# Retention outputs by three products of 64 columns, two heads in one PSUM bank, and the pooled low parts on GpSimd

## Chip, cores and metric

One core of one Trainium2 chip runs the whole kernel in one launch. The metric is the device time of the launch in microseconds (us), the median of the runs. The engines are TensorE (PE for its matmuls, PEld for its weight loads), VectorE (DVE), ScalarE (ACT), GpSimd (POOL), and SyncE (SP), which issues most transfers.

## The reference, cut to what matters

The reference is a two-layer backbone. Each layer projects the tokens into three head groups (retention, latent attention, pooling), joins them by an output projection, and runs a gated MLP with a depthwise convolution. There are 1024 latent tokens and 256 context tokens; the last layer has outputs for latent tokens alone. The part in question is retention, with 4 heads of key width 32 and value width 64:

```python
def step(s, inp):
    qi, ki, vi = inp
    a = jnp.einsum('bhqd,bhkd->bhqk', qi, ki) * dmat
    o = jnp.einsum('bhqk,bhkv->bhqv', a, vi) + jnp.einsum('bhqd,bhdv->bhqv', qi * q_dec, s)
    ...
fwd = retention_chunkwise(q, k, v, log_gf, s_f, True)
bwd = retention_chunkwise(jnp.flip(q, 2), jnp.flip(k, 2), jnp.flip(v, 2), log_gb, s_b, False)
...
o = o * lax.rsqrt(jnp.mean(o * o, axis=-1, keepdims=True) + NORM_EPS)
return (merge_heads(o) * jax.nn.silu(g.astype(jnp.float32))).astype(g.dtype)
```

## The kernel before

All large products run on values that are split into a high and a low part (fp32r), so that one product of two values is a sum of several matmuls. The layers follow one another, and in each layer the stages follow in the order of the code: projections, retention states, `retention(l)`, attention, output projection, MLP. Instructions stay on each engine in the order in which the code issues them; the framework adds the semaphore waits that the tiles' readers and writers need.

`retention(l)` (L1511) works in **units**, one for a head h and a block j of 256 query tokens. Units come in pairs that share j: the even head first, the odd head second. Layer 0 has 20 units (16 with j < 4, and 4 of context tokens with j = 4, which have no state part), layer 1 has 16. Unit u issues, in this order:

- `low(u+1)` (L1555): the low part of the next unit's decayed scores, on GpSimd for an odd u+1, on VectorE for an even one.
- the output matmuls into a PSUM tile O: 4 with the states as weights (O<-qd, L1600) and 4 with the values as weights (O<-Ahl, L1605). The weights have 128 columns, the 64 high ones beside the 64 low ones, so that O has the products with the high halves in partitions 0 to 63 and those with the low halves in 64 to 127.
- `qk(u+2)`: two score matmuls (L1540) and on VectorE the product with the decay table into af (L1543).
- if one is left, one of five pieces of `values` (six matmuls of 512 columns into vps, L1287; then ve on ScalarE, L1292, and on VectorE, L1293).
- at u = 6 (`POOL0`) `pooled()` puts ten splits of the pooled outputs into a list (`later`); each call of `tick` runs as many of them as its credit pays for (1.5 a unit, and a split costs 0.6). A split is a copy on ScalarE (yp, L178) and a subtraction on VectorE (yp, L179).
- `ot` (L1623): ScalarE copies partitions 64 to 127 of O; `high(u+2)` (L1552) makes the next scores' high part on ScalarE; then VectorE adds the two halves of O into `ops` (L1626).
- after the odd head of a block, `finish` queues the block's norm: steps of squares and gate (acc L458 on ScalarE, L1565 on GpSimd), sums (rps, two matmuls or more, L138), roots (rs, L148 and L151), spread (Rps, eight matmuls for 512 tokens, L159), `out` and `low`. One step runs per unit, with the gaps that `FINW` lists behind each step.

PSUM tiles of `self.pu` (O, qk, vps) rotate over six banks. The attention stage begins (SL) when the last units' `out` is there.

Of the kernel before, what the change touches and what calls it, by code (L numbers as in the profile page):

```python
# [8 lines left out]
F32 = mybir.dt.float32  # L9
F32R = mybir.dt.float32r  # L10
AF = mybir.ActivationFunctionType
ALU = mybir.AluOpType
# [15 lines left out]
CH_LAT = [(0, 512), (512, 512)]  # L28
SEG_ALL = [(0, SEQ), (SEQ, CTX)]
SEG_LAT = [(0, SEQ)]  # L30
FINW = (0, 0, 1, 0, 0, 0)
POOL0 = 6

LAST = [(0, 512), (512, 256), (768, 256)]
# [127 lines left out]
class Net:  # L162
# [1348 lines left out]
    def retention(self, l):  # L1511
        nc = self.nc
        gv, v, R = self.gv, self.v, self.ret
        lat = l == L - 1
        Tq, chq = self.Tq, self.chq
        NJ = Tq // 256
        Y = self.Y = [None] * 16

        def pooled():

            for i in range(2):
                Y[6 + i], Y[14 + i] = (self.slot(s + i, [128, Tq], F32R, "yp") for s in (6, 14))
                for c0, n in chq:
                    self.later(0.6, lambda i=i, c0=c0, n=n: self.split(Y[6 + i][:, c0:c0 + n], Y[14 + i][:, c0:c0 + n],
                                                                       self.yp[:, i, c0:c0 + n]))

        js = (0, 1, 2, 3) + ((4,) if not lat else ())
        units = [(h, j) for i in range(2) for j in js for h in (2 * i, 2 * i + 1)]
        ops = [None, None]
        NU = len(units)  # L1530

        af, A = {}, {}

        def qk(u):
            h, j = units[u]
            q, k = R.st[h]
            ps = self.pu.tile([128, 512], F32, tag="up", name="qk")
            for i in range(2):
                c = (2 * j + i) * 128
                nc.tensor.matmul(ps[:, i * 256:i * 256 + 256], k[:, c:c + 128], q[:, j * 256:j * 256 + 256],  # L1540
                                 start=True, stop=True)
            af[u] = gv.tile([128, 512], F32, tag="sq", name="af", bufs=2)
            nc.vector.tensor_tensor(out=af[u], in0=ps, in1=R.D[h], op=ALU.mult)  # L1543

        def high(u):
            if u % 3 == 2 and u >= NU // 2 + 5:

                self.run_to(1, pool_end)
                A[u] = self.gva.tile([128, 2, 512], F32R, tag="A", name="Ahl")
            else:  # L1550
                A[u] = self.slot((22, 23, 16)[u % 3], [128, 2, 512], F32R, "Ahl")
            nc.scalar.activation(A[u][:, 0], af[u], AF.Copy)  # L1552

        def low(u):
            (nc.gpsimd if u % 2 else nc.vector).tensor_tensor(out=A[u][:, 1], in0=af.pop(u),  # L1555
                                                              in1=A[u][:, 0].bitcast(F32), op=ALU.subtract)

        def finish(i, c0, n):
            cs = slice(c0, c0 + n)
            t = {}  # L1560
            def sq():
                t["x"] = x = ops[i][:, cs]
                acc = self.sumsq([x], n, gv)
                t["r"] = Rms(self, acc, n, 1.0 / 64, R.sel)
                nc.gpsimd.tensor_tensor(out=x, in0=x, in1=self.gate[:, i, cs], op=ALU.mult)  # L1565
            def out():
                nc.vector.tensor_tensor(out=t["x"], in0=t["x"], in1=t["r"].R, op=ALU.mult)
                if Y[i] is None:
                    Y[i], Y[8 + i] = (self.slot(s, [128, Tq], F32R, "yr") for s in (i, 8 + i))
                nc.scalar.activation(Y[i][:, cs], t["x"], AF.Copy)  # L1570
            def low():
                nc.vector.tensor_tensor(out=Y[8 + i][:, cs], in0=t["x"], in1=Y[i][:, cs].bitcast(F32), op=ALU.subtract)
            st = [sq, lambda: t["r"].sums(), lambda: t["r"].roots(), lambda: t["r"].spread(), out, low]
            fins.append([f for f, w in zip(st, FINW) for f in [f] + [None] * w])

        def fin_step():

            for f in list(fins):
                g = f.pop(0)
                if g:  # L1580
                    g()
                if not f:
                    fins.remove(f)
        fins = []

        qk(0)
        high(0)
        qk(1)
        high(1)
        low(0)  # L1590
        for u, (h, j) in enumerate(units):
            if u + 1 < NU:
                low(u + 1)
            O = self.pu.tile([128, 512], F32, tag="up", name="O")[:, 0:256]
            first = True
            if j < 4:
                r = slice(32 * h, 32 * h + 32)
                for d in range(2):
                    for p in range(2):
                        nc.tensor.matmul(O, R.S[d][j // 2][r, j % 2].rearrange("p s e -> p (s e)"),  # L1600
                                         R.qd[d][p][r, j * 256:j * 256 + 256], start=first, stop=False)
                        first = False
            for p in range(2):
                for i in range(2):
                    nc.tensor.matmul(O, v[:, 2 * j + i, h], A[u][:, p, i * 256:i * 256 + 256], start=first,  # L1605
                                     stop=p == 1 and i == 1)
                    first = False
            if u + 2 < NU:
                qk(u + 2)
            if self.values:  # L1610
                self.values.pop(0)()
                if not self.values:
                    R.stack(2)
                    R.stack(3)
            if u == POOL0:
                pooled()
                pool_end = self.added[1]
            self.tick(1.5)
            i = h // 2
            if ops[i] is None:  # L1620
                ops[i] = self.slot((17, 13)[i], [128, Tq], F32, "op")
            t = gv.tile([64, 256], F32, tag=("krt", "kr2")[u % 2], name="ot")
            nc.scalar.activation(t, O[64:128], AF.Copy)  # L1623
            if u + 2 < NU:
                high(u + 2)
            nc.vector.tensor_tensor(out=ops[i][64 * (h % 2):64 * (h % 2) + 64, j * 256:j * 256 + 256], in0=O[0:64],  # L1626
                                    in1=t, op=ALU.add)
            if h % 2 == 1:

                if j == 4 or j > 1 and lat and i:  # L1630
                    finish(i, j * 256, 256)
                elif j % 2:
                    finish(i, j * 256 - 256, 512)
            fin_step()
        self.run_all()
        while fins:
            fin_step()


    def attention(self, l):  # L1640
# [4 lines left out]
        with ExitStack() as es:  # L1645
# [143 lines left out]
            def av(u, g):  # L1789
                s = st[u]  # L1790
                v = heads[units[u][0]][2]
                if g == 0:
                    s.O = self.b([128, 512], "O")
                if g < 2 and not units[u][2]:
                    return
                f = 8 if not units[u][2] else 0
                for k in ((0, 1, 2, 3), (4, 5, 6, 7), (8, 9))[g]:
                    nc.tensor.matmul(s.O[:, 0:256], v[:, k], s.ph[:, k], start=k == f, stop=False)  # L1798
                    nc.tensor.matmul(s.O[:, 0:256], v[:, k], s.pl[:, k], start=False, stop=k == 9)  # L1799
# [480 lines left out]
```

## Time and profile before

| what | us |
|---|---|
| median of 3 runs | 3344.43 |
| the runs | 3340.59, 3344.43, 3345.43 |
| the profiled execution's own time | 3334.97 |
| its span | 3333.2 |
| PE busy in it | 3171.5 (95%) |
| DVE busy | 2143.8 (64%) |
| ACT busy | 1291.3 (39%) |
| POOL busy | 413.1 (12%) |

Times of single instructions come from the profiled execution, which was 9.46 us below the median. The retention units lie at about 416 to 493 us (layer 0) and 2150 to 2213 us (layer 1) of its span. A PE row of several matmuls (x4) gives the time from the first's start to the last's end; matmuls are pipelined, so the distance of two starts, and not one's duration, is what one costs in a dense stream.

### The profile page before, as it was taken

To read this page: it belongs to the slowest core of one execution; us is meant where nothing else is said; L and a number is where in the kernel's file an instruction comes from. 1 tells how busy PE (TensorE), PEld (TensorE's weight loads), DVE (VectorE), ACT (ScalarE), POOL (GpSimd) and SP (SyncE) were. 2 spreads that over 40 slices of the span, in tenths; PEclk is the share of its full clock that TensorE was granted. 3 is DMA by queue.
4 is the path that set the end of the run, shared out by engine and by line. 5 is a ranking of instruction groups with operands and counts; after the bars stand their busy time and mean duration, and the time that the engine had idled before them with its cause. 6 is when DMAs were issued, how large, how long until landed. Compare 5 with 4: busy or idle time off the path is not lost.

```text
span 3333.2 us, 43486 instructions
## 1 busy us (share of the span) xinstructions
PE 3171.5 (95%) x16873; PEld 2676.0 (80%) x16873; DVE 2143.8 (64%) x3720; ACT 1291.3 (39%) x2277; POOL 413.1 (12%) x557
## 2 busy tenths in 40 slices
PE   7989789999999999999999899789999999999998
PEld 4767668998878888888888787579988788888887
DVE  6434768987667666666665745669985655555556
ACT  7443447774332222222222423457762422222222
POOL 3550221121310000000000300221112100000000
PEclk8999869999999999999999999879999999999999
DMA  6531643222212222222221322542223111111111
GB/s 227 178 120 52 243 114 82 64 67 99 76 46 62 64 64 64 64 64 64 64 64 39 105 88 85 205 117 77 68 85 89 58 48 48 48 48 48 48 48 73
DMA packets 307464, 280.27 MB, mean 84 GB/s; under 512 B 28880, under 2 KB 274874, under 8 KB 307258
## 3 DMA queue, kind: packets, MB, share of 16 engines
q1 hardware_dynamic: 292778, 228.65, 23.3%
q0 software_dynamic: 9152, 35.91, 2.7%
q10 hardware_dynamic: 5328, 12.93, 1.0%
q8 instruction: 133, 2.18, 0.3%
q14 instruction: 73, 0.60, 0.1%
HBM read 219.51 MB, written 57.93 MB: 83 GB/s over the span
## 4 chain that ended last, share of the span: by engine, by line
PE 78%; DVE 10%; ACT 5%; issue 3%; POOL 2%; DMA 2%; SPq 0%; DVEq 0%; POOLq 0%; ACTq 0%
PE up L203 30%; PE ip L826 8%; PE dn L189 5%; PE dn L190 5%; PE dn L191 5%; PE pt L1745 4%; PE O L1798 2%; PE O L1799 2%; PE SL L189 2%; PE SL L190 2%; PE SL L191 2%; PE wo L189 2%; PE wo L191 2%; PE wo L190 2%; DMA mraw<-in_w_mod_dram 1%
## 5 line engine op out<-in xcount | busy, mean ns | idle before, releaser
L2086 DVE SCALAR_TENSOR_TENSOR x<-dn,mod,x 128x512 f32<-128x512 f32 (+1 forms) x448 | 306.1, 687 | 401.8 <-PE dn L191 401.4
L189 PE MATMUL dn<-ah,dh 128*128 128x512 f32 (+1 forms) x800 | 295.2, 369 | 2.6 <-DVE x L2086 2.6
L190 PE MATMUL dn<-al,dh 128*128 128x512 f32 (+1 forms) x800 | 294.7, 368 | 0.0
L191 PE MATMUL dn<-ah,dl 128*128 128x512 f32 (+1 forms) x800 | 294.4, 368 | 0.0
L203 PE MATMUL up<-yml,whi 128*128 128x512 f32 (+1 forms) x840 | 254.6, 368 | 0.0
L203 PE MATMUL up<-ym,wlo 128*128 128x512 f32 (+1 forms) x840 | 254.4, 368 | 0.0
L203 PE MATMUL up<-ym,whi 128*128 128x512 f32 (+1 forms) x840 | 254.4, 368 | 0.0
L2037 ACT ACTIVATE t<-up,vecs 128x1280 f32<-128x1280 f32 (+2 forms) x92 | 116.0, 1265 | 307.6 <-PE up L203 297.6
L2046 DVE SCALAR_TENSOR_TENSOR t<-up,vecs,t 128x1023 f32<-128x1023 f32 (+2 forms) x135 | 134.4, 995 | 144.4 <-ACT t L2037 144.3
L203 PE MATMUL up<-yp,whi 128*128 128x512 f32 (+1 forms) x840 | 220.6, 369 | 0.0
L203 PE MATMUL up<-yr,whi 128*128 128x512 f32 (+1 forms) x840 | 215.0, 370 | 5.1 <-ACT whi L178 5.1
L1766 DVE TENSOR_TENSOR ptl<-pt,pth 128x512 fp32r<-128x512 f32 x328 | 214.3, 681 | 1.3 <-ACT pth L1761 0.2
L251 POOL TENSOR_TENSOR wlo<-raw,whi 128x512 fp32r<-128x512 f32 (+1 forms) x10 | 16.4, 1659 | 1579.7 <-ACT whi L250 1579.7
L1761 ACT ACTIVATE pth<-pt 128x512 fp32r<-128x512 f32 x328 | 184.7, 600 | 44.1 <-PE pt L1745 40.7
L179 DVE TENSOR_TENSOR wlo<-raw,whi 128x1024 fp32r<-128x1024 f32 (+1 forms) x134 | 163.6, 1221 | 56.4 <-ACT whi L178 56.4
L1745 PE MATMUL pt<-cpack,P 128*128 128x128 f32 x1312 | 180.9, 275 | 3.6 <-DVE op L1822 2.5
L402 DVE SCALAR_TENSOR_TENSOR macc<-mraw,sc,macc 128x128 f32<-128x128 f32 x560 | 175.1, 357 | 7.0
L203 PEld LDWEIGHTS up<-ym,wlo 128*128 128x128 f32 x840 | 158.4, 189 | 26.2
L203 PEld LDWEIGHTS up<-ym,whi 128*128 128x128 f32 x840 | 158.4, 189 | 26.2
L203 PEld LDWEIGHTS up<-yml,whi 128*128 128x128 f32 x840 | 158.3, 189 | 26.0
L189 PEld LDWEIGHTS dn<-ah,dh 128*128 128x128 f32 x800 | 150.7, 188 | 32.9 <-issue 5.6
L203 PEld LDWEIGHTS up<-yr,whi 128*128 128x128 f32 x840 | 150.9, 189 | 30.7 <-ACT whi L178 5.9
(405 smaller groups left out, 7661.8 us busy)
## 6 DMA issues: line engine op xcount, KB each, us to landing
raw<-in_w_up_dram SPq DMA_DIRECT2D x88, 512.0 KB
mraw<-in_w_mod_dram SPq DMA_DIRECT2D x56, 512.0 KB
draw<-in_w_down_dram SPq DMA_DIRECT2D x80, 256.0 KB
mraw<-in_w_mod_dram SPq DMA_DIRECT2D x96, 128.0 KB
raw<-in_w_in_dram SPq DMA_DIRECT2D x22, 512.0 KB
vsp<-ve POOLq DMA_DIRECT2D x20, 512.0 KB, 3.0
kh<-ksp SPq DMA_DIRECT2D x32, 320.0 KB
vh<-vsp SPq DMA_DIRECT2D x16, 640.0 KB
```

Of the source, the lines that this page charges most:

```text
L179: self.nc.vector.tensor_tensor(out=lo, in0=src, in1=hi.bitcast(F32), op=ALU.subtract)
L189: mm(ps, wh, rh, start=first, stop=False)
L190: mm(ps, wh, rl, start=False, stop=False)
L191: mm(ps, wl, rh, start=False, stop=last)
L203: mm(ps[:, c0:c0 + n], w(k), r(k)[:, c0:c0 + n], start=k == 0 and i == 0, stop=k == K - 1 and i == 2)
L402: nc.vector.scalar_tensor_tensor(out=acc[:, v], in0=raw[:, k], scalar=self.sc[:, k, v:v + 1], in1=acc[:, v], op0=ALU.mult, op1=ALU.add)
L826: mm(ps[:, c0:c0 + n], x, y[:, c0:c0 + n], start=j == 0, stop=j == 3 * K - 1)
L1745: nc.tensor.transpose(ps[:, i], s.P[tt][:, k * 128:k * 128 + 128], self.ident)
L1761: nc.scalar.activation(hi, ps, AF.Copy)
L1766: nc.vector.tensor_tensor(out=lo, in0=ps, in1=hi.bitcast(F32), op=ALU.subtract)
L2046: stt(out=t[:, f:e], in0=ps[:, f - 1:e - 1], scalar=V.cw0[:, m:m + 1], in1=t[:, f:e], op0=ALU.mult, op1=ALU.add)
L2086: stt(out=x, in0=ps, scalar=g2[:, m, v:v + 1], in1=x, op0=ALU.mult, op1=ALU.add)
```

## The change

Each unit now uses weights of 64 columns and three products instead of four: high with high, high with low, low with high. That makes 12 output matmuls for a unit with j < 4 (before 8), and 6 for one with j = 4 (before 4). O needs no adding of halves; the `ot` copy and the VectorE add are gone. Both heads of a pair write one tile of one bank, partitions 0 to 63, the even head columns 0 to 255, the odd one 256 to 511. The even head's O is copied to `ops` by VectorE, the odd head's by ScalarE. The pooled low parts move from VectorE to GpSimd, and `tick` gives a credit of 0.7 instead of 1.5 a unit, so that about one split falls to a unit. `FINW` gets a gap of one unit between the squares and the sums.

```diff
-FINW = (0, 0, 1, 0, 0, 0)
+FINW = (1, 0, 1, 0, 0, 0)
...
-                    self.later(0.6, lambda i=i, c0=c0, n=n: self.split(Y[6 + i][:, c0:c0 + n], Y[14 + i][:, c0:c0 + n],
-                                                                       self.yp[:, i, c0:c0 + n]))
+                    self.later(0.6, lambda i=i, c=slice(c0, c0 + n): parts(i, c))
+
+        def parts(i, c):
+            nc.scalar.activation(Y[6 + i][:, c], self.yp[:, i, c], AF.Copy)
+            nc.gpsimd.tensor_tensor(out=Y[14 + i][:, c], in0=self.yp[:, i, c], in1=Y[6 + i][:, c].bitcast(F32),
+                                    op=ALU.subtract)
...
-            O = self.pu.tile([128, 512], F32, tag="up", name="O")[:, 0:256]
-            first = True
+
+            g = h % 2
+            if g == 0:
+                pair = self.pu.tile([128, 512], F32, tag="up", name="O")
+            O = pair[0:64, 256 * g:256 * g + 256]
+            todo = []
             if j < 4:
                 r = slice(32 * h, 32 * h + 32)
                 for d in range(2):
-                    for p in range(2):
-                        nc.tensor.matmul(O, R.S[d][j // 2][r, j % 2].rearrange("p s e -> p (s e)"),
-                                         R.qd[d][p][r, j * 256:j * 256 + 256], start=first, stop=False)
-                        first = False
-            for p in range(2):
+                    for e, p in ((0, 0), (0, 1), (1, 0)):
+                        todo.append((R.S[d][j // 2][r, j % 2, e], R.qd[d][p][r, j * 256:j * 256 + 256]))
+            for p, e in ((0, 0), (0, 1), (1, 0)):
                 for i in range(2):
-                    nc.tensor.matmul(O, v[:, 2 * j + i, h], A[u][:, p, i * 256:i * 256 + 256], start=first,
-                                     stop=p == 1 and i == 1)
-                    first = False
+                    todo.append((v[:, 2 * j + i, h, 64 * e:64 * e + 64], A[u][:, p, i * 256:i * 256 + 256]))
+            for n, (x, y) in enumerate(todo):
+                nc.tensor.matmul(O, x, y, start=n == 0, stop=n == len(todo) - 1)
...
-            self.tick(1.5)
+            self.tick(0.7)
...
-            t = gv.tile([64, 256], F32, tag=("krt", "kr2")[u % 2], name="ot")
-            nc.scalar.activation(t, O[64:128], AF.Copy)
             if u + 2 < NU:
                 high(u + 2)
-            nc.vector.tensor_tensor(out=ops[i][64 * (h % 2):64 * (h % 2) + 64, j * 256:j * 256 + 256], in0=O[0:64],
-                                    in1=t, op=ALU.add)
+            op = ops[i][64 * g:64 * g + 64, j * 256:j * 256 + 256]
+            if g == 0:
+                nc.vector.tensor_copy(op, O)
+            else:
+                nc.scalar.activation(op, O, AF.Copy)
```

On TensorE, from the last piece of unit 0's values on, unit 1 (an odd head) stood in the program before the change as follows (vps are the values, O<-qd the state part, O<-Ahl the part within the chunk, qk the scores of unit 3):

```order
L1287 MATMUL vps<-wlo,ch 128x512
L1600 MATMUL O<-qd,ssp 128x256 x4
L1605 MATMUL O<-Ahl,v 128x256 [waits Activation_49]
L1605 MATMUL O<-Ahl,v 128x256
L1605 MATMUL O<-Ahl,v 128x256 [waits Pool_49]
L1605 MATMUL O<-Ahl,v 128x256
L1540 MATMUL qk<-qst,kst 128x256 [waits PE_49]
```

and in the changed program:

```order
L1287 MATMUL vps<-wlo,ch 128x512
L1613 MATMUL O<-qd,ssp 64x256 [waits DVE_49]
L1613 MATMUL O<-qd,ssp 64x256 x5
L1613 MATMUL O<-Ahl,v 64x256 [waits Activation_49]
L1613 MATMUL O<-Ahl,v 64x256 x3
L1613 MATMUL O<-Ahl,v 64x256 [waits Pool_49]
L1613 MATMUL O<-Ahl,v 64x256
L1544 MATMUL qk<-qst,kst 128x256 x2
```

Eight matmuls have become twelve, and the first of them now waits for VectorE. Every odd unit has such a wait on its first output matmul, in units with j = 4 on the first O<-Ahl.

On VectorE the work around the first units was, before (from the low part of unit 0 on):

```order
L1555 TENSOR_TENSOR Ahl<-af,Ahl 128x512 [waits DMAHW6_49,Activation_49]
L1543 TENSOR_TENSOR af<-qk,D 128x512 [waits DVE_49,PE_49]
L1293 TENSOR_TENSOR ve<-vps,ve 128x8x64 [waits DMASW1_49,Activation_49]
L1626 TENSOR_TENSOR op<-O,ot 64x256 [waits Activation_49]
L1555 TENSOR_TENSOR Ahl<-af,Ahl 128x512 [waits Activation_49]
L1543 TENSOR_TENSOR af<-qk,D 128x512 [waits PE_49,Pool_49]
```

and is now:

```order
L1559 TENSOR_TENSOR Ahl<-af,Ahl 128x512 [waits DMAHW6_49,Activation_49]
L1547 TENSOR_TENSOR af<-qk,D 128x512 [waits DVE_49,PE_49]
L1293 TENSOR_TENSOR ve<-vps,ve 128x8x64 [waits DMASW1_49,Activation_49]
L1632 COPY op<-O 64x256
L1559 TENSOR_TENSOR Ahl<-af,Ahl 128x512 [waits Activation_49]
L1547 TENSOR_TENSOR af<-qk,D 128x512 [waits PE_49,Pool_49]
```

The copy of the even head's output has the place of the add: behind `af` of the unit after next and behind `ve` of the values that the unit issued.

On GpSimd the low parts from unit 7's on stood, before, beside the gate's products alone:

```order
L1555 TENSOR_TENSOR Ahl<-af,Ahl 128x512 [waits Activation_49]
L1565 TENSOR_TENSOR op<-op,gate 128x512 [waits Activation_49]
L1555 TENSOR_TENSOR Ahl<-af,Ahl 128x512 [waits PE_49,Pool_49]
L1565 TENSOR_TENSOR op<-op,gate 128x256 [waits Activation_49]
L1555 TENSOR_TENSOR Ahl<-af,Ahl 128x512 [waits PE_49,Pool_49]
```

and now:

```order
L1559 TENSOR_TENSOR Ahl<-af,Ahl 128x512 [waits Activation_49]
L1528 TENSOR_TENSOR yp<-d,yp 128x512 [waits DMASW5_49,DMASW1_49,Activation_49]
L1528 TENSOR_TENSOR yp<-d,yp 128x512 [waits Activation_49]
L1528 TENSOR_TENSOR yp<-d,yp 128x256 [waits Activation_49]
L1569 TENSOR_TENSOR op<-op,gate 128x512 [waits DVE_49,Activation_49]
L1559 TENSOR_TENSOR Ahl<-af,Ahl 128x512 [waits DVE_49]
```

Three pooled low parts, those of units 6, 7 and 8, have come between unit 7's low part and unit 9's.

## Rows read from the trace of the kernel before

**Rows 1.** The page: busy time, share of the span and instructions of each engine.
```profile
PE 3171.5 (95%) x16873; PEld 2676.0 (80%) x16873; DVE 2143.8 (64%) x3720; ACT 1291.3 (39%) x2277; POOL 413.1 (12%) x557
```
**Rows 2.** Windows of the retention units: length, busy by engine, granted clock, DMA share, GB/s.
```profile
410.00:416.50 6.50, 5.54 (x23) 4.85 (x22) 5.36 (x16) 1.99 (x5) 2.53 (x2) 0.50 0.02 5
...
425.20:445.70 20.50, 19.59 (x112) 15.01 (x111) 12.62 (x21) 12.92 (x25) 7.83 (x9) 1.00 0.62 203
445.70:473.00 27.30, 23.40 (x95) 18.39 (x95) 21.07 (x35) 13.04 (x28) 8.67 (x7) 0.50 0.11 24
473.00:479.80 6.80, 6.55 (x42) 5.40 (x42) 4.95 (x9) 2.65 (x6) 1.31 (x1) 1.00 0.86 203
2155.80:2172.80 17.00, 16.32 (x92) 12.38 (x90) 11.16 (x19) 9.59 (x19) 6.93 (x9) 1.00 0.51 178
...
2186.50:2193.30 6.80, 6.31 (x44) 5.17 (x45) 5.16 (x9) 2.92 (x7) 1.56 (x1) 1.00 0.08 11
```
**Rows 3.** Timeline of PE, layer 0, unit 3: start, us, instruction, idle before.
```profile
431.34 0.74 PE L1600 MATMUL O<-qd,ssp 32*128 32x256 f32 x4
...
434.32 0.38 PE L1600 MATMUL O<-qd,ssp 32*128 32x256 f32 x1
```
**Rows 4.** Timeline of DVE at the same place.
```profile
432.08 0.69 DVE L1293 TENSOR_TENSOR ve<-vps,ve 128x512 fp32r<-128x512 f32 x1 [1.12 <-ACT ve L1292]
432.69 0.41 DVE L1626 TENSOR_TENSOR op<-O,ot 64x256 f32<-64x256 f32 x1
```
**Rows 5.** Timeline of all engines, units 6 and 7, no values left.
```profile
440.18 0.74 PE L1600 MATMUL O<-qd,ssp 32*128 32x256 f32 x4
440.35 0.69 DVE L1543 TENSOR_TENSOR af<-qk,D 128x512 f32<-128x512 f32 x1 [0.35 <-PE qk L1540]
...
441.75 0.38 PE L1600 MATMUL O<-qd,ssp 32*128 32x256 f32 x1
```
**Rows 6.** Timeline of a unit in the window of granted clock 0.50.
```profile
465.59 1.22 PE L1600 MATMUL O<-qd,ssp 32*128 32x256 f32 x4
...
468.33 0.58 PE L1600 MATMUL O<-qd,ssp 32*128 32x256 f32 x1
```
**Rows 7.** Timeline of PE in attention: two matmuls of 64 columns of weights, then the next.
```profile
2232.08 0.40 PE L1806 MATMUL O<-dg,onesr 128*64 128x256 f32 x2
2232.31 0.28 PE L1798 MATMUL O<-pth,vh 128*128 128x256 f32 x1
```
**Rows 8.** Timeline of PE ahead of the first unit.
```profile
415.38 0.41 PE L190 MATMUL U<-v,kdh 128*128 128x256 f32 x1
415.60 0.41 PE L191 MATMUL U<-v,kdl 128*128 128x256 f32 x1
```
**Rows 9.** Weight loads of the tiles named O: ns min/median/max, first and last start.
```profile
L1605 PEld LDWEIGHTS O<-Ahl,v x144: 186/189/338, 421.1 to 2203.6; 128*128 128x128 f32 x144
...
L1806 PEld LDWEIGHTS O<-dg,onesr x144: 133/134/138, 513.3 to 2488.9; 128*64 128x64 f32 x144
```
**Rows 10.** Groups by line, shapes apart, DVE copies from PSUM: busy us, mean ns | idle.
```profile
L660 DVE COPY x<-xps 128x256 f32<-128x256 f32 x7 | 2.6, 413 | 0.0
```
**Rows 11.** Waits of PE, 440 to 493 us: us in total, times, longest.
```profile
PE rps L138 <- ACT acc L458: 4.1, 3, 1.4
PE O L1605 <- DVE Ahl L1555: 2.1, 1, 2.1
```
**Rows 12.** Waits of PE, 2150 to 2213 us.
```profile
PE qk L1540 <- DMA kst<-rksp: 4.7, 2, 3.3
```
**Rows 13.** Timeline of all engines, layer 0, 444 to 455 us.
```profile
444.41 1.15 PE L159 MATMUL Rps<-rs,selT 32*128 32x128 f32 x8 [0.54 <-DVE rs L151]
...
446.29 1.29 DVE L179 TENSOR_TENSOR yp<-d,yp 128x512 fp32r<-128x512 f32 x2 [1.39 <-DMA vsp<-ve]
...
451.24 1.27 POOL L1565 TENSOR_TENSOR op<-op,gate 128x512 f32<-128x512 f32 x1 [8.18 <-ACT acc L458]
...
451.71 2.75 DVE L179 TENSOR_TENSOR yp<-d,yp 128x512 fp32r<-128x512 f32 x2 [0.49 <-ACT yp L178]
```

## Prediction

> **What bounds the kernel now.** I read the page's busy times first: TensorE works 95% of the span, no other engine more than 64% [rows 1]. So the change is priced by what it does to TensorE's stream in the retention units, and by what TensorE waits for there. Work that other engines lose counts only where TensorE waits for it. Next come windows of those stretches: what the reader is to see there is the granted clock, which is 1.00 in four windows (20.5, 6.8, 17.0 and 6.8 us, 51.1 together) and 0.50 between the first two and ahead of the first unit [rows 2]. In the stretch at 0.50 TensorE was busy 23.4 of 27.3 us, in the first full one 19.6 of 20.5. Then the timeline gives the price of a unit. At full clock, without values, it lasts from 440.18 to 441.75, 1.57 us [rows 5]; at half clock one lasts from 465.59 to 468.33, 2.74 us [rows 6]; one with a piece of values, at full clock, from 431.34 to 434.32, 2.98 us [rows 3]. Last come the waits of TensorE: in layer 0 4.1 us in three waits of the sums (rps) for the squares on ScalarE and 2.1 us in one for a low part on VectorE [rows 11], in layer 1 4.7 us in two for keys that a transfer brings [rows 12].
>
> **More matmuls.** Layer 0 has 16 units with 12 instead of 8 and 4 with 6 instead of 4, layer 1 has 16 with 12: 72 + 64 = 136 more. Does a matmul whose weights have half as many columns cost less? The trace has such ones: two start at 2232.08 and the next matmul at 2232.31, 0.115 us each [rows 7], with 256 columns to move as here. So three products cost 12/8 of four. At half clock two matmuls of 256 columns are 415.38 and 415.60, so 0.22 us apart [rows 8, 2]. All 136 at full clock are 15.6 us, all at half 29.9. I take a third at full clock, since about that share of the stretch will keep it (below): 45 x 0.115 + 91 x 0.22 = 25.2. The weight loads go the other way: 134 ns for 64 columns against 189 [rows 9]. They lie beside the matmuls, and PEld is less busy than PE in each window [rows 2], so that between nothing and 136 x 0.055 = 7.5 us comes back; I take 3. **Term A: +22 (8 to 30).**
>
> **The second head's wait.** The program puts a wait for VectorE on the first output matmul of each odd unit: it shares its bank with the even head, whose output VectorE has still to copy. That copy stands behind `af` and, where there is one, behind `ve`; TensorE runs in order, so `qk` of the unit after next and all behind it stand too. The nearest row for the copy, 128x256 out of PSUM, is 413 ns [rows 10]; the add that had its place took 0.41 [rows 4].
>
> With values: before, the next unit began at 431.34, and the instruction in the copy's place ran from 432.69, behind `ve` of 432.08, to 433.10 [rows 3, 4]. The wait is 1.76 us, 1.8 with the signal. Units 0, 2 and 4 of each layer have values, so it comes 6 times. **Term B: +10.8 (9 to 13).**
>
> Without values: the unit at 440.18 would wait for `af`, which begins at 440.35 and lasts 0.69, and then for 0.41 of copy: until 441.45, 1.27 us [rows 5], taken as 1.3. That is the wait of 12 pairs (7 in layer 0, 5 in layer 1), 15.6 in all. With the new gap in `FINW` the spreads (Rps) come at the end of even units, ahead of the wait; eight of them took 1.15 us [rows 13], so they fill nearly all of one wait, in about 6 pairs. **Term C: 6 x 1.3 = +7.8 (4 to 15.6).** Nothing is removed for it: `ot` and the add, now gone, were awaited by no TensorE instruction of these units.
>
> **Waits that go.** The sums come one unit later, so that the squares are there: 4.1. The low part that came late stood behind pooled subtractions on VectorE (446.29 and 1.29 us long for two) [rows 13]; these leave VectorE: 2.1 [rows 11]. **Term D: -6.2 (-6.2 to 0).** In layer 1 TensorE comes to the late keys some 5 us or more later by terms A and B, and they don't come later for it unless their buffers do: **term E: -4.4 (-4.7 to 0).**
>
> **Pooled low parts on GpSimd.** A subtraction of 128x512 there is bounded by the 1.27 us of the gate's product [rows 13] and by half as much again, 1.9. Ten of these spread over ten units of 1.6 to 4 us fit in GpSimd's idle time (7.8 of 20.5 us busy in the busiest window [rows 2]). TensorE waits for GpSimd only if an odd unit's low part comes late; it is issued a unit ahead, and odd units start late anyway. I take nothing; if that cover is gone, up to 10 x 0.4 = 4. VectorE may be slowed: beside the gate's product two subtractions took 2.75 us, against 1.29 for two alone [rows 13]. The Trainium skill has a reason (SBUF — State Buffer, section "Who interferes with whom"): a VectorE instruction with both inputs in SBUF and a GpSimd instruction that reads SBUF block one another. The trace agrees, 2.75 against 1.29 us; by the rule the low parts of even units would each wait for a pooled one at times, which I would estimate at up to 4 us more, and the sum leaves it out.
>
> **The clock.** The clock fell where TensorE had paused: 444.41 ends such a pause (0.54) [rows 13], and from 445.70 it is 0.50 [rows 2]. The change puts a pause of 1.3 to 1.8 us into every other unit, so some of the 51.1 us at full clock will run at half. A unit then takes 2.74 for 1.57, 0.745 us more for each. A third of 51.1 lost: 17 x 0.745 = 12.7. **Term F: +12.7 (-10 to +35).** From below: the removed waits stood at half clock, and 13 us of that might come back to full, 13 x 0.745. From above: nearly all is lost.
>
> **The end of the stage.** Attention waits for the last `out`. There a copy replaces `ot` and the add (-0.4), and the sums come a unit later (+0.5): nothing.
>
> **Sum:** 22 + 10.8 + 7.8 - 6.2 - 4.4 + 12.7 = 42.7, on the profiled execution's 3334.97: 3377.7. That execution lies 9.46 below the median shown, so beside the runs it is 3344.4 + 42.7 = **3387**.
>
> **Rivals.** Each time is put against the median.
>
> 1. *The clock holds.* TensorE has more to do between its pauses, 12 for 8 matmuls, and the longer waits are gone. Then A is 15.6 - 3 = 12.6, and of the stretch at half clock some 8 us turn full (F = -6): 12.6 + 10.8 + 7.8 - 6.2 - 4.4 - 6 = +14.6, **3359**. For it speaks that full windows have pauses too (17.0 us with 16.3 busy [rows 2]); against it, that those are short.
> 2. *The clock is lost and the keys come as late as before.* A 29.9 - 3 = 26.9, C 15.6, E 0, F two thirds of 51.1 x 0.745 = 25.4: 26.9 + 10.8 + 15.6 - 6.2 + 25.4 = +72.5, **3417**. For it: buffers of the keys come free with the scores, which move along.
> 3. *The other side: the second head is not held up,* because in steady state the copy is done when TensorE arrives (VectorE runs ahead, the matmuls of the even head are longer). Then B and C are nothing, A is 12.6, D and E as above, and without pauses 13 us at half clock turn full (-10): 12.6 - 6.2 - 4.4 - 10 = -8, **3336**. It decides when the 18 waits are under 8/18 = 0.44 us each. Against it: `af`, which stands ahead of the copy, needs `qk`, which is the last matmul ahead of the waiting one, so that 0.69 + 0.41 is a floor but for what stands between.
> 4. *TensorE's extra work is hidden,* since something else ends these stages, and the kernel does not change: **3344**. TensorE's 19.6 of 20.5 us [rows 2] speaks against it.
>
> The Trainium skill says (PSUM — Partial Sum Buffer, section "PSUM bank collisions raise a hardware error") that a matmul's writes and another engine's reads in one bank and one quarter of the partitions have to be kept apart by semaphores, whatever the columns. By it the wait of rival 3 can't be absent, only short; no run here shows a collision, and the chances stand without it.
>
> **How the numbers follow.** Forecast 0.57, rival 1 0.18, rival 2 0.13, rival 3 0.07, rival 4 0.05. The forecast's own range is +28 to +58 (F from 0 to 25, C from 6 to 11). The range reaches down to rival 1 with some room and up to near rival 2: 3354 to 3413; outside are rivals 3 and 4 (0.12) and about half of rival 2. A measurement of this kernel can tell about 0.2%, 6.7 us, from no change. Faster by more than that is rival 3, 0.07; within it rival 4, 0.05; slower the rest, 0.88.
>
> **What would show it.** A: 136 more output matmuls, 0.115 us apart at full clock, 0.22 at half. B and C: waits of TensorE for a VectorE copy, near 1.8 us six times and 1.3 us or less twelve times, 12 to 25 us in all; less than 8 in all makes rival 3. D: no waits of rps for acc. E: the wait for keys in layer 1 under 1 us. F: the clock in the windows of the units, full for about 34 us. Late low parts on GpSimd would show as waits of output matmuls for POOL above the few now. The prediction is wrong if the copies come before TensorE needs them, or if the clock is at 1.00 through most of the units.

## The result and the profile after

The changed kernel takes 3379.93 us (median of 4 runs, 3375.86 to 3384.06) against 3344.18 for the kernel before: a ratio of 1.0109, 95% interval 1.0091 to 1.0126, so 30 to 42 us slower. The forecast was 3387 us, its range 3354 to 3413. The profiled execution took 3377.71, close to its median; that of before, 3334.97, was the quickest seen of its kernel. Single executions of one kernel differ by up to 20 us here (early_fin0 below, 3336 to 3356), so sizes below come from medians and ratios; single rows show places and mechanisms.

The page of the changed kernel, busy time by engine, answers to [rows 1]:

```profile
PE 3206.8 (95%) x17009; PEld 2706.0 (80%) x17009; DVE 2132.4 (63%) x3692; ACT 1284.2 (38%) x2259; POOL 424.5 (13%) x567
```

TensorE has exactly 136 matmuls more and is busy 35 us longer. The span grew by 42.7 us (3333.2 to 3375.9). Where? Windows from the first output matmul of each layer to attention's first, for the kernel before and then the changed one (length, busy by engine, granted clock, DMA share, GB/s):

```profile
416.80:492.90 76.10, 63.18 (x291) 48.45 (x290) 49.63 (x84) 35.60 (x74) 23.63 (x22) 0.68 0.36 103
2147.30:2212.70 65.40, 52.98 (x252) 40.60 (x251) 39.78 (x70) 29.87 (x61) 20.27 (x19) 0.71 0.42 122
```

```profile
418.40:518.30 99.90, 81.01 (x363) 63.30 (x362) 43.04 (x72) 32.29 (x63) 30.64 (x28) 0.64 0.28 79
2173.60:2256.00 82.40, 68.82 (x316) 53.90 (x315) 35.25 (x57) 26.97 (x53) 24.84 (x23) 0.64 0.31 89
```

The retention units became 23.8 and 17.0 us longer, 40.8 of the 42.7. TensorE's busy time in them grew by 33.7 (116.2 to 149.8), its idle time by 7.1 (25.3 to 32.5). The mean clock fell a little, to 0.64 in both.

TensorE's waits in those stretches, layer 0 and then layer 1 (us in total, times, longest), answer to [rows 11, 12]:

```profile
PE O L1613 <- DVE op L1632: 8.5, 6, 1.7
PE O L1613 <- POOL Ahl L1559: 3.4, 2, 2.5
...
PE rps L138 <- ACT acc L458: 0.6, 1, 0.6
```

```profile
PE O L1613 <- DVE op L1632: 7.9, 6, 1.7
PE Rps L159 <- DVE rs L151: 1.4, 1, 1.4
...
PE SL L189 <- DVE op L1571: 0.6, 1, 0.6
```

The wait for the copy is there, 12 times and 16.4 us in all, and is the largest. The waits of the sums fell from 4.1 to 0.6 us in layer 0, and the 4.7 us for keys in layer 1 are gone. The timeline shows one wait of each kind. First behind a piece of values, at the start of unit 1:

```profile
428.33 0.60 ACT L1292 ACTIVATE ve<-vps 128x512 fp32r<-128x512 f32 x1 [4.07 <-PE vps L1287]
...
428.96 0.69 DVE L1293 TENSOR_TENSOR ve<-vps,ve 128x512 fp32r<-128x512 f32 x1 [2.50 <-ACT ve L1292]
429.57 0.41 DVE L1632 COPY op<-O 64x256 f32<-64x256 f32 x1
...
430.03 0.91 PE L1613 MATMUL O<-qd,ssp 32*64 32x256 f32 x6 [1.74 <-DVE op L1632]
```

VectorE's copy needs only the output matmuls, which were done long before; it comes at 429.57 because it stands behind `ve`. TensorE idles for 1.74 us. Without values the copy stands behind `af`:

```profile
456.85 0.69 DVE L1547 TENSOR_TENSOR af<-qk,D 128x512 f32<-128x512 f32 x1 [4.13 <-PE qk L1544]
457.45 0.41 DVE L1632 COPY op<-O 64x256 f32<-64x256 f32 x1
...
457.91 1.54 PE L1613 MATMUL O<-qd,ssp 32*64 32x256 f32 x6 [1.10 <-DVE op L1632]
...
459.38 1.54 PE L1613 MATMUL O<-Ahl,v 128*64 128x256 f32 x6
```

VectorE had been idle for 4.13 us, so it was not too busy: it waited for the scores, TensorE's last work ahead of the waiting matmul. In layer 0 the four odd units that do not wait for the copy each have a spread (Rps) ahead of them, at 462.78, 482.41, 490.31 and 504.27, as forecast.

What the output matmuls cost shows in units without a pause, from the first output matmul to the scores. The units of [rows 5] and [rows 6], which begin at 440.18 and 465.59, end before the change at

```profile
441.42 0.40 PE L1540 MATMUL qk<-qst,kst 96*128 96x256 f32 x2
...
467.76 0.63 PE L1540 MATMUL qk<-qst,kst 96*128 96x256 f32 x2
```

and the two units above, from 430.03 (granted clock 1.00) and from 457.91 (0.50), at

```profile
431.64 0.54 PE L1544 MATMUL qk<-qst,kst 96*128 96x256 f32 x2
...
460.72 0.63 PE L1544 MATMUL qk<-qst,kst 96*128 96x256 f32 x2
```

Eight matmuls took 1.24 us at full clock and 2.17 at half, twelve take 1.61 and 2.81. So one with weights of 64 columns is cheaper than one with 128 (0.134 against 0.155 us, 0.234 against 0.271), and the four more of a unit cost 0.37 or 0.64 us. For all 136 that is 12.6 us at full clock and 21.8 at half.

### The profile page after: what moved, and what is told of

Same layout as the page of the kernel before. It is cut to its first block, busy times and chain, and to the rows that moved or that the text cites. A ratio compares the mean times of both kernels' runs of the same rounds, so it can differ in the third digit from the quotient of the medians.

```text
span 3375.9 us, 43704 instructions
## 1 busy us (share of the span) xinstructions
PE 3206.8 (95%) x17009; PEld 2706.0 (80%) x17009; DVE 2132.4 (63%) x3692; ACT 1284.2 (38%) x2259; POOL 424.5 (13%) x567
## 4 chain that ended last, share of the span: by engine, by line
PE 79%; DVE 10%; ACT 5%; issue 2%; DMA 2%; POOL 2%; SPq 0%; DVEq 0%; POOLq 0%; ACTq 0%
PE up L203 30%; PE ip L826 8%; PE dn L190 5%; PE dn L189 5%; PE dn L191 5%; PE pt L1752 4%; PE O L1805 2%; PE O L1806 2%; PE O L1613 2%; PE SL L189 2%; PE SL L191 2%; PE SL L190 2%; PE wo L189 2%; PE wo L191 2%; PE wo L190 2%
```

## The experiments

Each run lists its ratio to the kernel before in the same set of runs, with its 95% interval; "us" is (ratio - 1) x 3343, the loss against the kernel before. The interval of one loss is some 3 to 6 us either way, that of a difference of two losses some 4 to 7.

| kernel | median | ratio | us |
|---|---|---|---|
| changed kernel | 3379.93 | 1.0109 (1.0091 to 1.0126) | +36.4 |
| own12: a bank for each head | 3356.36 | 1.0041 (1.0027 to 1.0054) | +13.7 |
| shared8: eight matmuls | 3368.72 | 1.0081 (1.0067 to 1.0094) | +27.1 |
| own8: both | 3350.78 | 1.0026 (1.0016 to 1.0035) | +8.7 |
| early_act: copy earlier, on ScalarE | 3359.91 | 1.0051 (1.0038 to 1.0064) | +17.0 |
| fin_only: before, later sums | 3354.03 | 1.0030 (1.0018 to 1.0042) | +10.0 |
| pool_only: before, pooled on GpSimd | 3342.22 | 0.9998 (0.9989 to 1.0007) | -0.7 |
| pool_fin: before, both | 3349.17 | 1.0013 (1.0004 to 1.0022) | +4.3 |
| after_fin0: changed, old `FINW` | 3372.01 | 1.0088 (1.0075 to 1.0101) | +29.4 |
| early_fin0: early_act, old `FINW` | 3345.91 | 1.0009 (0.9998 to 1.0020) | +3.0 |
| three_only: before, three products, own banks | 3348.78 | 1.0023 (1.0013 to 1.0032) | +7.7 |

### Taking the wait away, taking the matmuls away

The theory was the prediction's: two costs that add, 136 matmuls and 18 waits. The main rival, A, was that the waits with the clock make nearly all of it.

**own12**, a bank for each head:

```diff
-            if g == 0:
+            if True:
                 pair = self.pu.tile([128, 512], F32, tag="up", name="O")
```

> The changed kernel with one edit: each head's O gets a bank of its own, so the second head of a pair does not wait for the copy of the first; the twelve matmuls of 64 columns stay. Theory (the loss is two things that add: 136 more matmuls, about 30 us, and 18 waits for the copy, about 16 us, less the waits that went): the waits of O for the copy go, 16 us come back, 3364 us (3358 to 3370). Rival A (the loss is the waits, mostly by the clock that they bring down): most of the loss goes, 3345 us or less, and the granted clock in the units is at least the 0.68 to 0.71 of before. Rival B (without the bank's wait the matmuls run into the next late operand, the low part on GpSimd or the scores' high part): 3376 us or more, with waits of O for POOL or ACT in place of those for DVE.

Waits of TensorE in layer 0:

```profile
PE O L1613 <- POOL Ahl L1559: 4.6, 3, 2.7
PE O L1613 <- DVE Ahl L1559: 4.2, 2, 3.3
```

The 16.4 us of waits for the copy are gone, and new ones for late low parts stand in their place in part; still the kernel gains 22.7 us, more than the theory's 16 and less than rival A's 35. The theory's range ends 2 us above the time, which the intervals can't tell from a hit (the waits were 12, not the 18 it counted). Rivals A and B (no gain) are out.

**shared8**, eight matmuls of 64 columns (the low halves of states and values are left out):

```diff
-                    for e, p in ((0, 0), (0, 1), (1, 0)):
+                    for e, p in ((0, 0), (0, 1)):
...
-            for p, e in ((0, 0), (0, 1), (1, 0)):
+            for p, e in ((0, 0), (1, 0)):
```

> The changed kernel with one edit: the product of the high part of the scores and queries with the low half of the weights stays, but that of the low scores or queries is cut as follows: the state part leaves out the low queries' half pair (high weights with both parts stay, low weights are left out), so eight matmuls of 64 columns a unit instead of twelve, four instead of six in a context unit; the low half of states and values is left out of the products. The bank stays shared. Theory: 136 matmuls at 0.22 us less, 30 us come back and the waits stay at 1.1 to 1.7 us each, since VectorE's copy waits for the scores and not for the matmuls: 3350 us (3343 to 3357). Rival A: the clock stays down with the waits, only 136 x 0.115 to 0.15 come back: 3362 us or more. Rival B (the matmuls are hidden behind VectorE's chain): the waits grow by what the matmuls give back, 3370 us or more.

Its windows and its waits in layer 0:

```profile
419.80:516.60 96.80, 74.52 (x292) 54.24 (x291) 41.60 (x72) 32.22 (x64) 31.23 (x28) 0.57 0.28 82
2172.30:2250.70 78.40, 61.41 (x252) 43.87 (x251) 36.03 (x57) 26.99 (x53) 24.77 (x23) 0.61 0.34 98
```

```profile
PE O L1613 <- DVE op L1632: 8.5, 6, 1.7
PE O L1613 <- POOL Ahl L1559: 5.2, 3, 1.8
```

136 matmuls less give back 9.3 us, a third of the theory's 30, though the price that the theory put on them holds here: eight of 64 columns take 1.13 or 1.95 us a unit, 0.48 or 0.86 less than twelve. The waits for the copy stay as they were (8.5 us in 6), as expected. Two things are seen to take from the gain, in one execution each: TensorE's idle time in the two stretches rises from 32.5 to 39.3 us (the waits for GpSimd's low parts alone from 3.4 to 5.2 in layer 0), and the clock falls from 0.64 to 0.57 and 0.61. The time is in what rival A allowed, but less came back than A's least, 15.6. Rival B's time, 3370 or more, is 1.3 us away; its growing waits for the copy are not there.

**own8**, both edits:

> Both edits: a bank for each head and eight matmuls of 64 columns (the low half of states and values is left out of the products). What is left of the change are the halves that need no adding, the pooled low parts on GpSimd and the later sums. Theory: 46 us come back against the changed kernel, that is 10 us faster than before by the waits for the squares and the keys that went: 3334 us (3328 to 3342). If the two losses share one part (the clock), it is less than the sum of what the two edits bring singly: the three results together tell how far they add.

With a bank for each head, the 136 matmuls are worth 5.0 us (13.7 against 8.7), which is not clear of noise by itself. TensorE's idle time rises without them here too, from 24.9 to 32.6 us. And the forecast of 3334 us failed: with no wait for the copy and no matmul too many, the kernel is still 8.7 us slower than before. Something else in the change costs as much as the matmuls.

**early_act** keeps the shared bank and moves the copy:

```diff
...
+            if g == 0:
+                nc.scalar.activation(op, O, AF.Copy)
             if u + 2 < NU:
                 qk(u + 2)
...
-            if g == 0:
-                nc.vector.tensor_copy(op, O)
-            else:
+            if g == 1:
                 nc.scalar.activation(op, O, AF.Copy)
```

> The changed kernel with the shared bank and the twelve matmuls, but the even head's output is copied by ScalarE, right behind its last output matmul in the program, ahead of the next scores, instead of by VectorE behind the decay product and the values. Theory: the copy takes 0.38 us and two score matmuls or six value matmuls lie beside it, so the waits fall from 1.1 to 1.7 us to 0.4 at most without values and to nothing with them: 3366 us (3360 to 3372), near the one with two banks. Rival B (ScalarE is late itself, behind the high part of the next scores and the pooled copies): the waits only change their name, 3376 us or more.

TensorE's waits for ScalarE's copy, layer 0 and (second fence) layer 1:

```profile
PE O L1613 <- ACT op L1619: 0.8, 2, 0.6
```

```profile
PE O L1613 <- ACT op L1619: 1.4, 3, 0.7
```

2.2 us of waits are left of 16.4, and 19.4 us come back, where 14 were expected (3366; measured 3359.9). Two different ways of removing the wait agree: it costs 19 to 23 us, 3 to 6 more than its own length, though a surplus of that size is within the intervals. By the windows TensorE's busy time for the same matmuls falls too, from 81.0 + 68.8 in the changed kernel to 78.0 + 62.0 here; that is where the surplus shows, though in one execution each.

### The other two edits alone

**fin_only** is the kernel before with `FINW = (1, 0, 1, 0, 0, 0)`.

> The kernel before with the later sums alone (FINW). Theory: the waits of the sums for the squares go, 4.1 us in layer 0 and 1.8 in layer 1, against 0.5 us at the end of each stage: 3339 us (3336 to 3344), not to be told from before with certainty. Rival (each gap only moves: the wait reappears at the spread or the end of the stage): 3344 us.

10.0 us slower: theory and rival both miss, the theory in the sign too. Its waits in layer 0, and the timeline around the longest:

```profile
PE O L1605 <- POOL Ahl L1555: 5.2, 4, 1.7
PE O L1605 <- DVE Ahl L1555: 4.4, 2, 4.1
...
PE rps L138 <- ACT acc L458: 0.8, 1, 0.8
```

```profile
446.22 1.29 DVE L179 TENSOR_TENSOR yp<-d,yp 128x512 fp32r<-128x512 f32 x2 [2.34 <-DMA vsp<-ve]
...
447.77 0.93 DVE L151 RECIPROCAL rs<-rs 32x128 f32<-32x128 f32 x1
448.62 0.62 DVE L1555 TENSOR_TENSOR Ahl<-af,Ahl 128x512 fp32r<-128x512 f32 x1
...
449.30 0.80 PE L1605 MATMUL O<-Ahl,v 128*128 128x256 f32 x2 [4.13 <-DVE Ahl L1555]
```

The sums no longer wait (4.1 to 0.8 us), but TensorE runs on into the next late thing. That is the low part on VectorE: 4.1 us, where it was 2.1 [rows 11]. It stands behind a pooled subtraction that waits for a transfer, and now also behind the root's reciprocal (0.93 us), which the gap has moved there. Waits for GpSimd's low parts are 5.2 us where layer 0 had 0.8 before:

```profile
PE O L1605 <- POOL Ahl L1555: 0.8, 3, 0.4
```

The three kinds together are 10.4 instead of 7.0 us. These waits do not make the whole 10.0: in both stretches together TensorE's idle time grows by 3.1 us (25.3 to 28.5). Its busy time grows by 10.4 (116.2 to 126.6), but part of that is the quick execution of before.

**pool_only** is the kernel before with the pooled part of the diff and `tick(0.7)`; **pool_fin** has both.

> The kernel before with the pooled low parts on GpSimd, one a unit, alone. Theory: the 2.1 us wait for the late low part of unit 8 goes, and one wait of up to 2.5 us for a low part on GpSimd comes, as in the changed kernel's trace: within 4 us of 3344. Rival (both low parts in one queue hold up odd units throughout): 3352 us or more, with O waiting for POOL many times.

> The kernel before with both, the later sums and the pooled low parts on GpSimd: the changed kernel without its matmuls and its shared bank. Theory: 3338 us (3333 to 3344), and the changed kernel's whole loss and more lies in the output matmuls and the copy's wait. Rival (GpSimd's and the sums' edits carry a part of the loss): 3350 us or more.

pool_only changes nothing that can be measured (-0.7 us). With both, the loss is 4.3 us, so on top of the pooled edit the later sums cost 5.0. pool_fin's time is the rival's (3350 or more; 3349.2), not the theory's 3338: the output part does carry most of the loss, but the rest does not help, it hurts. From pool_only to pool_fin the retention units became 7.2 us longer (146.6 to 153.8), and all of it is waiting: TensorE is busy 126 us in both.

### The sums and the matmuls once more

> The changed kernel with the gaps of the norm's steps as before, FINW (0, 0, 1, ...). Theory (the later sums cost what they cost in the kernel before, 10 us alone and 7 on top of the pooled edit, since the root's reciprocal then stands ahead of a low part that TensorE waits for): 3371 us (3367 to 3375). Rival (in the changed kernel the later spreads come ahead of the second head's matmuls and fill its wait, so that undoing this gives the waits back): 3384 us or more, with 18 waits of 1.1 to 1.7 us for the copy in place of the 12 or so now.

The changed kernel with the old `FINW` gains 7.0 us, just within the interval of that difference: the later sums seem to cost there too. The rival falls by its time, though its mechanism can be seen: the waits for the copy grow, in layer 0 from 8.5 to

```profile
PE O L1613 <- DVE op L1632: 12.5, 7, 3.5
```

while in layer 1 they fall from 7.9 to 6.9 in 5. They are 12 in all, as with the later sums, and 3.0 us longer: the shift had filled that much of them, and it did not pay. Its windows:

```profile
416.70:505.30 88.60, 69.77 (x363) 55.55 (x362) 42.14 (x68) 32.46 (x63) 30.05 (x28) 0.75 0.30 86
2162.30:2247.20 84.90, 71.08 (x316) 55.46 (x315) 34.45 (x57) 27.05 (x53) 24.82 (x23) 0.62 0.34 96
```

The later sums make these stretches 8.8 us longer (173.5 to 182.3), and here none of it is waiting (32.7 against 32.5 us): the same matmuls take 9.0 us more, at a lower clock.

> The changed kernel with the even head's output copied by ScalarE right behind its matmuls, and with the gaps of the norm's steps as before. Of the kernels with all three products it has the fewest waits that are known. Theory (wait and later sums add): 3360 less 7 to 10, 3352 us (3347 to 3356), still slower than before by what the 136 matmuls cost. Rival (with the copy early nothing waits for the later sums any more): 3360 us. A time of 3341 or less would make it a version that beats both kernels.

Three products, shared bank, early copy, old `FINW`: +3.0 us, the interval just reaching 1. Measured 3345.9, with 3352 expected: the later sums are worth 14.0 us here. Again it is mostly busy time: 10.4 (129.5 to 140.0) of the 12.0 us by which early_act's stretches are longer. It does not beat the kernel before.

**three_only** has the three products with a bank for each head and nothing else of the change.

> The kernel before with the three products alone: twelve matmuls of 64 columns a unit, a bank for each head, the copy on VectorE or ScalarE in place of the adding; pooled low parts, tick and FINW as before. What is left of the change is the price of 136 matmuls, less ot and the add. If a matmul more costs what it takes in the stream (0.115 to 0.22 us each): 3360 to 3374 us. If, as the runs with eight and twelve matmuls in banks of their own said (3351 against 3356), most of it goes into pauses that were there and into a clock that stays up: 3349 us (3345 to 3354).

7.7 us slower, as the second reading had it. Its windows, in an execution that like that of before was some 8 us under its median:

```profile
419.20:494.60 75.40, 60.90 (x363) 46.73 (x362) 46.42 (x77) 32.22 (x64) 24.57 (x22) 0.84 0.35 101
2150.00:2218.30 68.30, 56.39 (x316) 43.73 (x315) 36.56 (x62) 26.98 (x53) 19.88 (x19) 0.80 0.41 119
```

TensorE does 136 matmuls more than before in these stretches and is busy as long, 117.3 us against 116.2, with the clock at 0.84 and 0.80 instead of 0.68 and 0.71.

## Why the prediction was right, and where its steps were not

The time is in the range and 7 us from the forecast, and one of its two large mechanisms, the second head's wait, is there as described and is the largest cost. But the largest term of the sum, the matmuls, was too large by 13 to 17 us, and the waits that go had the wrong sign, and these cancelled: that the number came so close is luck. By the runs, one way through the change is: three products with an early copy, and the pooled edit, +3.0 (early_fin0); the wait for the copy, +26.4 (after_fin0); the later sums, +7.0. Intervals of each step are some 4 to 7 us either way, so that the last is not clear of noise by itself.

- **Term A, more matmuls (+22):** the count (136) is right. Three products were put at 12/8 of four; the units show 1.61 us against 1.24, 1.3 times, which at the forecast's third of full clock makes 18.7 instead of 22. The step that failed is that each matmul adds what it takes in the stream at the clock of before. Taken alone the products cost 7.7 (three_only). The low products alone are worth 5.0 (own12 against own8), with the shared bank 9.3. The values lie around the low end of its bounds, 8.
- **Terms B and C, the second head's wait (+18.6):** right in place and number. Six waits of 1.74 us were forecast as 1.8; of those without values six are left, five of 1.1 and one of 0.5, against 7.8 us forecast: 16.4 us altogether. What it costs by the runs is more, 19 to 26 us.
- **Term F, the clock (+12.7):** put in the wrong form. In the profiled executions a clock of 0.64 instead of 0.68 and 0.71 means 51 us at full clock instead of 55: 4 lost, not 17. All the added time ran at the lower clock instead. What can be called the clock's share of the wait is the 3 to 10 us by which removing it gives more than its length, as far as that is clear of noise.
- **Term D, waits that go (-6.2):** wrong in sign. The waits of the sums did go (4.1 to 0.6 us), and the step that failed is that they were counted as gained. In four pairs of kernels the later sums cost 5 to 14 us. With the four products of before TensorE came to late low parts sooner; with three products the time shows as the same matmuls at a lower clock, and why the later sums lower it stays open.
- **Term E, the keys (-4.4):** as forecast in the changed kernel's trace, where the wait is gone. In own12 it is back at 2.3 us: it was only covered by other waits.
- **Pooled low parts (nothing):** right, -0.7 us. The cover held not quite: a wait of 2.5 us for a low part on GpSimd came, inside the 4 us bound. The two subtractions of 2.75 us that the forecast read as lying beside the gate's product lay beside GpSimd's next low part too (from 452.47, 1.72 us).
- **Rivals:** rival 1 (the clock holds, +14.6) misses the time by 21 us; its matmuls (12.6) are nearer to the measured 5 to 9, but the clock and the waits that go, which it counted as gains, were none. Rival 3's condition, waits under 0.44 us, is met in early_act on the mean of 18 pairs (2.2 us in all); without the later sums the loss is then within the interval of nothing, and no gain. Rivals 2 and 4 fall by the times.

What stays open is how 136 matmuls are paid with 5 to 9 us. A part lies in pauses that are there anyway: without them TensorE idles 6.8 us longer in the shared bank and 7.7 us with own banks. Another part may be the clock. The windows show the clock higher with them (0.84 and 0.80 in three_only; 0.64 against 0.57 and 0.61 without them in the shared bank), but own12 against own8 shows no such order (0.69 and 0.63 against 0.63 and 0.67), in one execution each. The granted clocks of whole launches, as means of all runs, are 0.9679 in three_only against 0.9656 in the kernel before beside it, 0.9650 in own12 against 0.9640 in own8, and 0.9605 in the changed kernel against 0.9603 in shared8. The first difference is worth 8 us of 3347, an estimate for an engine that is always busy, against the 12.6 to 21.8 us that the rows ask for. So the clock was higher with the matmuls, clearly in the first pair; that it is the denser stream that holds it up is argued and not shown. The same means are lower with the later sums in all four pairs: 0.9632 against 0.9644, 0.9638 against 0.9647, 0.9605 against 0.9633, 0.9644 against 0.9695.

## What to carry to other kernels

A tile that two pieces of work share makes the second wait for the reader of the first: look at what that reader stands behind in its own queue, since the copy took 0.41 us and nearly every wait 1.1 to 1.7. Either give the second piece its own bank or issue the copy, on an idle engine, ahead of the long work; both gave back 19 us or more here. A wait that a shift removes is not a gain until the next operand is shown to be early, so test such a shift alone. And take the price of a matmul from the stream in which it will stand: a pair from another stage gave 1.5 times the work of before, the units themselves 1.3 times.

## What was not expected of the hardware

Matmul time was not a fixed price: the same stage took 679 matmuls in 117.3 us of busy time at clocks of 0.84 and 0.80, and 543 in 116.2 at 0.68 and 0.71. Both were quick executions of their kernels. Executions of one kernel spread with the clock: the 12 runs of three_only go from 3341 us at a mean granted clock of 0.973 to 3356 at 0.963.

VectorE's low parts became slower. Groups by line, the kernel before, then the changed one (busy us, mean ns | idle before):

```profile
L1555 DVE TENSOR_TENSOR Ahl<-af,Ahl 128x512 fp32r<-128x512 f32 x18 | 13.5, 749 | 1.7 <-ACT Ahl L1552 1.3
```

```profile
L1528 POOL TENSOR_TENSOR yp<-d,yp 128x512 fp32r<-128x512 f32 x8 | 10.0, 1268 | 3.6 <-ACT yp L1527 2.3 <-issue 1.4
...
L1559 DVE TENSOR_TENSOR Ahl<-af,Ahl 128x512 fp32r<-128x512 f32 x18 | 14.6, 810 | 2.5 <-ACT Ahl L1556 2.2
```

The pooled low parts on GpSimd do this alone (a mean of 845 ns in pool_only), but not they only: the later sums alone have 806 (fin_only). It is 1.1 us over 18 instructions in the changed kernel. That is under the 4 us that the forecast's estimate from the Trainium skill allowed (SBUF — State Buffer, section "Who interferes with whom").
